# The first FFN of a decoder trunk as 2x2 block products in seven products, on one core

## The chip, the cores and the metric

The kernel runs on one core of one Trainium2 chip. The metric is the device time of one execution in microseconds (us). TensorE (PE) multiplies, VectorE (DVE), ScalarE (ACT) and GpSimd (POOL) work on SBUF, DVE and ACT also read PSUM, and SyncE (SP) issues the DMAs.

## The reference, cut to what matters

```python
def swiglu(u, wg, wu, wd):
    return (jax.nn.silu(u @ wg) * (u @ wu)) @ wd

x = x + 0.5 * swiglu(rms_norm(x, norm_ffn1[i]), ffn1_gate[i], ffn1_up[i], ffn1_down[i])
x = x + mixer(rms_norm(x, norm_mix[i]), ...)            # SSD scan and pooling heads
x = x + 0.5 * swiglu(rms_norm(x, norm_ffn2[i]), ffn2_gate[i], ffn2_up[i], ffn2_down[i])
gate = jax.nn.sigmoid(rms_norm(x, norm_ple[i]) @ ple_gate[i])
x = x + gate * (p[i] @ ple_proj[i])
y = rms_norm(x, final_norm)
```

There are 1024 prompt tokens and 32 sample tokens, together T = 1056. The model width is 1024, the FFN width 2816, all in float32.

## The kernel before

**Layout.** Features lie on the 128 partitions, tokens along the free axis. The width of 1024 is 8 row blocks (KB), the FFN width 22 blocks of 128 (NF). Tokens go in three chunks, `CH`, of 384, 384 and 288 columns.

**Precision.** Each operand is split into an upper and a lower part, rounded for TensorE (type fp32r). A product is three matmuls: upper by upper, lower weights by upper activations, upper weights by lower activations (`three`, whose matmul is line L280). For a weight tile ACT makes the upper part (L244) and DVE the lower (L245); for the activations of a norm ACT L307 and DVE L308 do it, with the norm's gain.

**The FFN** (`ffn`). The gate of a block is 3 chunks of 24 matmuls, then the up of the block is 3 chunks of 24, 144 in all. DVE L356 takes a gate chunk out of PSUM times the norm's factor R, ACT L357 applies SiLU, POOL L358 multiplies by R; DVE L368 takes the up chunk out, ACT L369 and DVE L370 split the result into g. The down projection goes in 8 `GROUPS` of 2 or 3 blocks between the gates and ups: a chunk is 6 or 9 matmuls, and DVE L387 adds it to x. Its 24 chunks by 8 groups make 192 evictions in each FFN.

**PSUM** is 8 banks of 512 columns, each a tile of its own. `bank()` hands out 7 of them in turn (5 in the scan).

**The start.** `start` runs the first block while x and the first weights still land: it goes block by block of the rows, with six banks open, and after each row the engines make the next operands. DVE and POOL add up the squares for the norm (L413); `finish_norm` (PE L322, ACT L323, DVE L325 to L327) makes R, which the first evictions need.

**Order.** PE's order is as the code is written (`MAN`); DVE, ACT and POOL are put in order by a scheduler except where the manual part of the program (`MS`) sets it. Weights come through a stream with `next_w`: one DMA of 512 KB (SP, L225) for each tile of gate or up, 256 or 384 KB for each pair of down tiles.

Of the kernel before, what the change touches and what calls it, by code (L numbers as in the profile page):

```python
# [78 lines left out]
def emit(tc, dr):  # L79
# [8 lines left out]
    # ---- SBUF: what stays for the whole run, and a pool for each phase  # L88
# [12 lines left out]
    o_X = new(sb, "X", 16 * T, F32R)     # [8][2][T], operands split in two parts  # L101
# [16 lines left out]
    banks = [pp.tile([P, 512], F32, name=f"bank{i}") for i in range(8)]  # L118
# [24 lines left out]
    # ---- the stream of weights, in the order of use  # L143
# [38 lines left out]
    ffn_stream("wgu1", "wd1")  # L182
# [68 lines left out]
    def first_w(q):  # L251
        """a quarter of the first two tiles"""
        for i in range(2):
            ap, n, _ = stream[i]
            o_r, o_w, k = raws[i] + n // 4 * q, where[i] + n // 4 * q, n // 4
            SY.dma_start(f(o_r, k), ap[:, k * q : k * q + k])
            S.copy(r(o_w, k), f(o_r, k))
            V.tensor_tensor(r(o_w + n, k), f(o_r, k), f(o_w, k), op=ALU.subtract)
            held[i] = i
            ready[i] = (where[i], n)  # L260
        st["made"], st["loaded"] = 2, 2
# [12 lines left out]
    def three(ps, terms):  # L274
        """ps = sum of w @ x over the terms ((wh, wl), (xh, xl)), without the product of the lower parts"""
# [65 lines left out]
    # ---- FFN  # L341
# [49 lines left out]
    # ---- FFN 1  # L391
    def start():
        for kb in range(KB):
            src = f(L["x"] + kb * T, T)
            if kb == 0:
                cuts = [(0, CH[0][1]), (CH[1][0], T - CH[1][0])]
            else:
                cuts = [(0, T)]
            for c0, n in cuts:
                SY.dma_start(src[:, c0 : c0 + n], dr["xT"][:, kb, c0 : c0 + n])  # L400
                if kb % 2 == 0 and c0 == 0:
                    first_w(kb // 2)
                split_gain(o_X + (2 * kb * T + c0), o_X + ((2 * kb + 1) * T + c0), src[:, c0 : c0 + n], vec(V_FFN1 + kb), n)
            acc = f(L["acc"], T)
            if kb == 0:
                S.activation(acc, src, AF.Square)
            else:
                sq = f((o_sq, o_T)[kb % 2], T)
                if kb in (1, 3):
                    V.tensor_tensor(sq, src, src, op=ALU.mult)  # L410
                else:
                    S.activation(sq, src, AF.Square)
                (G if kb < 5 else V).tensor_tensor(acc, acc, sq, op=ALU.add)  # L413
        SY.dma_start(f(o_cst, C_N), dr["cst"])
        V.tensor_copy(r(o_rii, P), cst(C_ID, P))
        V.tensor_copy(r(o_rii + P, P), cst(C_ID, P))
        wg, wu = next_ws(2)
        pss = [[bank()[:, 0:n] for c0, n in CH] for _ in range(2)]
        later_norm(o_R0, True)
        for kb in range(KB):  # L420
            for i, (p, q) in enumerate(((0, 0), (1, 0), (0, 1))):
                for w, pw in zip((wg, wu), pss):
                    for (c0, n), ps in zip(CH, pw):
                        PE.matmul(ps, lhsT=w(kb, p), rhs=Xs(kb, q, c0, n), start=kb == 0 and i == 0, stop=kb == KB - 1 and i == 2)  # L424
                if kb == KB - 1 and i < 2:
                    for c0, n in CH[i : 2 * i + 1]:
                        Rn(o_R0, c0, n)
        return pss

    o_sq = new(ph_acc, "sq", T)  # L430
# [6 lines left out]

    def done1(m, c0, n):
        src = f(L["x"] + m * T + c0, n)
        next_norm(o_R0, V_MIX, m, c0, n, src)  # L440
        if c0 + n == T:
            SY.dma_start(d_x[:, m, :], f(L["x"] + m * T, T))

    def before1():
        less_w(2)
        st["leaves"] = L["raw"]
        if L["raw"] in raws:
            raws.remove(L["raw"])

    ffn(o_R0, done1, start, before1)  # L450
# [3 lines left out]
    # ---- pooling heads  # L454
    ph_ffn.release()
# [6 lines left out]
    def pool_in(m):  # L462
# [678 lines left out]
```

## Time and profile before

| | |
|---|---|
| median of three runs | 2425.45 us (2424.33 to 2428.67) |
| span of the profiled execution | 2425.2 us |
| PE busy | 2350.8 us, 97% of the span |
| DVE busy | 1202.8 us, 50% |
| ACT busy | 680.9 us, 28% |
| POOL busy | 484.9 us, 20% |

The profiled execution is one of the kind that was timed; its span is 0.25 us below the median. The busy shares are means over the whole span: stages with different limits lie behind them. "PE" counts a matmul from its start to the end of its drain, so it can be busy and yet not at its best pace; the pace is read from a stretch divided by its matmuls.

### The profile page before, as it was taken

To read this page: it belongs to the slowest core of one execution; us is meant where nothing else is said; L and a number is where in the kernel's file an instruction comes from. 1 tells how busy PE (TensorE), PEld (TensorE's weight loads), DVE (VectorE), ACT (ScalarE), POOL (GpSimd) and SP (SyncE) were. 2 spreads that over 40 slices of the span, in tenths; PEclk is the share of its full clock that TensorE was granted. 3 is DMA by queue.
4 is the path that set the end of the run, shared out by engine and by line. 5 is a ranking of instruction groups with operands and counts; after the bars stand their busy time and mean duration, and the time that the engine had idled before them with its cause. 6 is when DMAs were issued, how large, how long until landed. Compare 5 with 4: busy or idle time off the path is not lost.

```text
span 2425.2 us, 34578 instructions
## 1 busy us (share of the span) xinstructions
PE 2350.8 (97%) x14259; PEld 2295.7 (95%) x14259; DVE 1202.8 (50%) x1912; ACT 680.9 (28%) x1132; POOL 484.9 (20%) x415
## 2 busy tenths in 40 slices
PE   8999999999999999999878999999999999999997
PEld 8999999999999999977767889999999999999997
DVE  7442433333245875555888774344333332433766
ACT  5111111111114224323443543311111112111555
POOL 3001000010103420013545435101000101000343
PEclk9999999999999999999999999999999999999999
DMA  4111111111112333344344664311111111111244
GB/s 151 49 57 39 54 40 46 51 42 53 38 44 89 75 92 70 52 124 138 113 144 133 186 185 128 127 53 57 40 46 51 44 50 38 49 48 44 64 140 130
DMA packets 135150, 192.36 MB, mean 79 GB/s; under 512 B 54672, under 2 KB 95952, under 8 KB 134992
## 3 DMA queue, kind: packets, MB, share of 16 engines
q1 hardware_dynamic: 134992, 190.15, 25.8%
q8 instruction: 112, 1.84, 0.3%
q14 instruction: 46, 0.38, 0.1%
HBM read 154.33 MB, written 35.78 MB: 78 GB/s over the span
## 4 chain that ended last, share of the span: by engine, by line
PE 85%; DVE 7%; ACT 2%; DMA 2%; issue 2%; POOL 1%; SPq 0%; DVEq 0%; POOLq 0%; ACTq 0%
PE bank L280 81%; PE bank L843 1%; DVE yol L821 1%; DVE X L308 1%; DVE wl L831 1%; PE bank L810 1%; ACT X L307 1%; DMA tmp<-d_z 1%; PE bank L424 1%; DMA x<-xT 1%; PE bank L322 0%; DVE x L387 0%; PE bank L747 0%; DVE W L245 0%; DVE Wa L687 0%
## 5 line engine op out<-in xcount | busy, mean ns | idle before, releaser
L280 PE MATMUL bank<-X,W 128*128 128x384 f32 (+1 forms) x9168 | 1505.7, 325 | 11.2 <-ACT X L882 4.6
L280 PEld LDWEIGHTS bank<-X,W 128*128 128x128 f32 x9168 | 1487.9, 189 | 16.6 <-ACT X L882 5.0
L280 PE MATMUL bank<-g,W 128*128 128x384 f32 (+1 forms) x3264 | 534.6, 324 | 2.1 <-ACT g L991 1.7
L280 PEld LDWEIGHTS bank<-g,W 128*128 128x128 f32 x3264 | 529.6, 188 | 2.9 <-ACT g L991 2.0
L358 POOL TENSOR_TENSOR tmp<-tmp,R 128x384 f32<-128x384 f32 x132 | 135.4, 1027 | 1302.7 <-ACT tmp L357 1302.7
L244 ACT CAST W<-raw 128x1024 fp32r<-128x1024 f32 (+2 forms) x230 | 211.1, 921 | 639.3 <-PE bank L280 608.9
L387 DVE SCALAR_TENSOR_TENSOR x<-bank,x 128x384 f32<-128x384 f32 (+1 forms) x384 | 198.6, 522 | 187.4 <-PE bank L280 187.3
L245 DVE TENSOR_TENSOR W<-raw,W 128x1024 fp32r<-128x1024 f32 (+2 forms) x230 | 250.1, 1090 | 65.0 <-ACT W L244 65.0
L356 DVE TENSOR_TENSOR tmp<-bank,R 128x384 f32<-128x384 f32 x132 | 68.9, 524 | 340.4 <-PE bank L280 340.3
L368 DVE TENSOR_TENSOR tmp<-bank,tmp 128x384 f32<-128x384 f32 x132 | 69.3, 525 | 289.3 <-PE bank L280 286.3
L369 ACT CAST g<-tmp 128x384 fp32r<-128x384 f32 x132 | 64.2, 487 | 342.8 <-DVE tmp L368 342.8
L357 ACT ACTIVATE tmp<-tmp 128x384 f32<-128x384 f32 x132 | 65.4, 498 | 328.1 <-DVE tmp L356 328.1
L316 POOL TENSOR_TENSOR acc<-acc,tmp 128x384 f32<-128x384 f32 (+1 forms) x82 | 84.2, 1035 | 94.7 <-ACT tmp L315 86.9
L280 PE MATMUL bank<-yh,W 128*128 128x384 f32 (+1 forms) x384 | 94.0, 330 | 0.0
L370 DVE TENSOR_TENSOR g<-tmp,g 128x384 fp32r<-128x384 f32 x132 | 68.9, 523 | 49.4 <-ACT g L369 49.4
L280 PEld LDWEIGHTS bank<-yh,W 128*128 128x128 f32 x384 | 68.5, 192 | 1.0 <-issue 0.6
L280 PE MATMUL bank<-yl,W 128*128 128x384 f32 (+1 forms) x192 | 62.6, 326 | 0.0
L308 DVE SCALAR_TENSOR_TENSOR X<-x,vec,X 128x384 fp32r<-128x384 f32 (+3 forms) x57 | 53.8, 949 | 17.1 <-ACT X L307 16.8
L650 DVE SCALAR_TENSOR_TENSOR cv<-xb,vec,cv 128x1080 f32<-128x1080 f32 x36 | 48.3, 1341 | 2.5 <-ACT cv L648 2.1
L787 POOL TENSOR_TENSOR Wa<-Wa,sm 128x1024 f32<-128x1024 f32 x16 | 49.5, 3092 | 0.0
L810 PE MATMUL bank<-xde,bt 128*128 128x512 f32 x32 | 20.9, 742 | 27.3 <-DVE xD L702 25.4
L307 ACT ACTIVATE X<-x,vec 128x384 fp32r<-128x384 f32 (+3 forms) x57 | 37.6, 661 | 31.7 <-DVE x L387 29.4
(230 smaller groups left out, 1600.9 us busy)
## 6 DMA issues: line engine op xcount, KB each, us to landing
raw<-wgu SPq DMA_DIRECT2D x86, 512.0 KB, 3.5
raw<-wd SPq DMA_DIRECT2D x48, 384.0 KB, 3.0
raw<-win SPq DMA_DIRECT2D x28, 512.0 KB, 4.9
raw<-ple SPq DMA_DIRECT2D x24, 512.0 KB, 3.7
Wa<-d_ac SPq DMA_DIRECT2D x16, 512.0 KB, 3.8
raw<-wout SPq DMA_DIRECT2D x16, 512.0 KB, 4.0
tmp<-d_x SPq DMA_DIRECT2D x32, 192.0 KB, 2.5
d_x<-tmp SPq DMA_DIRECT2D x32, 192.0 KB, 2.4
```

The costliest lines, as they stand in the source:

```text
L244: S.copy(r(o_w, n), f(o_r, n))
L245: V.tensor_tensor(r(o_w + n, n), f(o_r, n), f(o_w, n), op=ALU.subtract)
L280: PE.matmul(ps, lhsT=a, rhs=b, start=i == 0, stop=i == n - 1)
L308: V.scalar_tensor_tensor(r(o_lo, n), src, gain, f(o_hi, n), op0=ALU.mult, op1=ALU.subtract)
L316: eng.tensor_tensor(f(L["acc"] + c0, n), f(L["acc"] + c0, n), f(o_q, n), op=ALU.add)
L356: V.tensor_tensor(f(t, n), ps, Rn(o_R, c0, n), op=ALU.mult)
L357: S.activation(f(t, n), f(t, n), AF.Silu)
L358: G.tensor_tensor(f(t, n), f(t, n), f(o_R + c0, n), op=ALU.mult)
L368: V.tensor_tensor(f(t, n), ps, f(t, n), op=ALU.mult)
L369: S.copy(r(o_hi, n), f(t, n))
L370: V.tensor_tensor(r(o_lo, n), f(t, n), f(o_hi, n), op=ALU.subtract)
L387: V.scalar_tensor_tensor(xm, ps, 0.5, xm, op0=ALU.mult, op1=ALU.add)
```

## The change

**Seven products.** For one FFN block, gate and up over the two halves of the 1024 rows (weights) and the two halves of the tokens (528 each) are a 2x2 block product. Before it was 144 matmuls a block, of 384 and 288 columns. Now it is 7 products (`product`) of 24 matmuls of 264 columns (L451), 168 in a block; a product fills two banks, each with 4 pairs of row blocks by 3 matmuls. Operands are sums and differences: of the activations once, at the start (`operands`: seven pieces of 528 columns for each of 4 pairs of row blocks, each split in two), of the weights for each block (`make_unit`: POOL L434 to L436 add, ACT L439 and DVE L440 split; 8 slots for the units, one raw load of 1 MB for each block). The results are put together from three PSUM pairs by DVE (L474 to L488), after ACT has copied the first product out (L472).

**PSUM.** For the whole program the eight banks are now halves of four tiles of 1024 columns, `pairs`. `bank()` is as it was.

**Through HBM.** The FFN's result goes to `d_h` in HBM. After all 22 blocks `ffn_b` reads it back (`load_g`) and does the down projection in 4 `KGROUPS` of 5 or 6 blocks: 24 chunks of 15 or 18 matmuls each, 96 evictions (L544) in place of 192. x is loaded a second time.

The second FFN's code, the mixer's and the end's are unchanged but for the banks.

```diff
-    banks = [pp.tile([P, 512], F32, name=f"bank{i}") for i in range(8)]
+    pairs = [pp.tile([P, 1024], F32, name=f"bank{i}") for i in range(4)]
+    banks = [pairs[i // 2][:, 512 * (i % 2) : 512 * (i % 2) + 512] for i in range(8)]
+    d_h = dp.tile([P, NF, T], F32, name="d_h")
...
+    def operands(q, x1, x2, v_gain, o_b2, o_nd, o_u, o_e, o_f):
+
+        g1, g2 = vec(v_gain + 2 * q), vec(v_gain + 2 * q + 1)
+        u, e, fq, b2, nd = f(o_u, TH), f(o_e, TH), f(o_f, TH), f(o_b2, T), f(o_nd, T)
+        parts(0, q, x1[:, 0:TH], g1)
+        S.activation(b2, x2, AF.Copy, scale=g2)
+        G.tensor_tensor(u, x1[:, 0:TH], x1[:, TH:T], op=ALU.subtract)
+        V.scalar_tensor_tensor(e, u, g1, b2[:, TH:T], op0=ALU.mult, op1=ALU.add)
+        parts(1, q, e)
+        parts(2, q, b2[:, 0:TH])
+        V.scalar_tensor_tensor(nd, x1, g1, b2, op0=ALU.mult, op1=ALU.subtract)
+        G.tensor_tensor(fq, nd[:, TH:T], nd[:, 0:TH], op=ALU.subtract)
+        parts(3, q, nd[:, TH:T])
+        parts(4, q, u, g1)
+        parts(5, q, fq)
+        parts(6, q, b2[:, TH:T])
...
+        if u == 0:
+            G.tensor_tensor(f(o_s, 1024), f(o_raw, 1024), f(o_raw + 512, 1024), op=ALU.add)
+            G.tensor_tensor(f(o_s + 1024, 512), f(o_raw + 1024, 512), f(o_s, 512), op=ALU.add)
+            G.tensor_tensor(f(o_s + 1536, 512), f(o_raw + 1536, 512), f(o_s + 1024, 512), op=ALU.add)
+        where_, c = U_SRC[u]
+        src, o = (o_raw if where_ == "raw" else o_s) + c, unit_at(i)
+        S.copy(r(o, 512), f(src, 512))
+        V.tensor_tensor(r(o + 512, 512), f(src, 512), f(o, 512), op=ALU.subtract)
+        if u == 5 and fb + 1 < NF:
+            load_raw(a, fb + 1)
+
+    def product(pair, o, i, first):
+        w = unit_at(i)
+        for h in range(2):
+            ps = pair[:, 512 * h : 512 * h + CQ]
+            for q in range(4):
+                x = piece(o, q) + CQ * h
+                for j, (p, b) in enumerate(((0, 0), (1, 0), (0, 1))):
+                    PE.matmul(ps, lhsT=r(w + (512 * p + P * q), P), rhs=r(x + TH * b, CQ),
...
+        for fb in range(NF):
+            o_g, o_c, o_u1, o_u2 = (L7["cg"] + ((fb % 2) * 4 + k) * TH for k in range(4))
+            for s in range(7):
+                i = 7 * fb + s
+                product(pairs[(0, 1, 0, 1, 2, 1, 2)[s]], s, i, s in (0, 1, 4))
+                if fb == 0 and s == 0:
+                    for c0, n in CH:
+                        Rn(o_R, c0, n)
+                make_unit(a, i + NU)
+                if s == 0:
+                    S.copy(p1, pa)
+                elif s == 1:
+                    V.tensor_tensor(v2, p1, px, op=ALU.subtract)
...
```

**Three places of the order.** The rows stand in the order in which an engine goes through them; "waits" names the engines whose signals the row waits for, and "x5" stands for five equal rows. On PE, in the down projection of the second FFN, before (bank_74 to bank_81 are the eight PSUM tiles, each one bank):

```order
L280 MATMUL bank_80<-g_11605,W_72 128x384 [waits DVE_49]
L280 MATMUL bank_80<-g_11605,W_72 128x384 x5
L280 MATMUL bank_74<-g_11605,W_72 128x384 [waits DVE_49]
L280 MATMUL bank_74<-g_11605,W_72 128x384 x5
L280 MATMUL bank_75<-g_11605,W_72 128x288 [waits DVE_49]
L280 MATMUL bank_75<-g_11605,W_72 128x288 x5
```

The same place now (bank_74 to bank_77 are the four pairs, each with two banks):

```order
L274 MATMUL bank_74<-g_12395,W_72 128x384 x6
L274 MATMUL bank_74<-g_12395,W_72 128x288 [waits DVE_49]
L274 MATMUL bank_74<-g_12395,W_72 128x288 x5
L274 MATMUL bank_75<-g_12395,W_72 128x384 x6
L274 MATMUL bank_75<-g_12395,W_72 128x384 [waits DVE_49]
L274 MATMUL bank_75<-g_12395,W_72 128x384 x5
L274 MATMUL bank_76<-g_12395,W_72 128x288 x6
L274 MATMUL bank_76<-g_12395,W_72 128x384 [waits DVE_49,Activation_49]
L274 MATMUL bank_76<-g_12395,W_72 128x384 x5
L274 MATMUL bank_77<-g_12395,W_72 128x384 x6
```

Before, each chunk's first matmul waited for the eviction that had emptied its own bank seven chunks earlier. Now the first chunk of a pair has no wait for DVE, and the second waits; the signal's count that is compiled into that wait is that of the eviction of the chunk just ahead, in the other half of the same tile.

On ACT, in the loop over the FFN's blocks, before (W are weight tiles, raw what was loaded, tmp a chunk of the gate or up, g the result):

```order
L357 ACTIVATE tmp_69<-tmp_69 128x384 [waits DVE_49] x2
L244 CAST W_12_93<-raw_14_95 128x1024 [waits DMAHW7_49,PE_49,Activation_49]
L357 ACTIVATE tmp_69<-tmp_69 128x288 [waits DVE_49]
L369 CAST g_92<-tmp_69 128x384 [waits DVE_49] x2
L244 CAST W_13_94<-raw_70 128x1024 [waits DMAHW0_49,PE_49,Activation_49]
```

And now (ws are the sums of weights that POOL makes, cg the FFN's results, p the copy of the first product):

```order
L439 CAST W_14_116<-ws_117 128x512 [waits PE_49,Pool_49]
L439 CAST W_14_116<-raw_70 128x512 [waits DMAHW1_49,PE_49,Activation_49]
L490 ACTIVATE cg_121<-cg_121 128x528 [waits Pool_49]
L439 CAST W_14_116<-ws_117 128x512 [waits PE_49,Activation_49,Pool_49]
L472 COPY p_16_118<-bank_74 128x528 [waits Activation_49]
L439 CAST W_14_116<-raw_70 128x512 [waits PE_49]
```

A cast that waits for the next block's load, and a cast that waits for POOL's sums of that load, now stand ahead of the copy that empties the first product's pair.

On POOL, at the start, before (acc is the norm's sum; the rows after these belong to the first gate):

```order
L413 TENSOR_TENSOR acc_99<-acc_99,tmp_69 128x1056 [waits DVE_49,Activation_49]
L413 TENSOR_TENSOR acc_99<-acc_99,sq_115 128x1056 [waits Activation_49,Pool_49]
L413 TENSOR_TENSOR acc_99<-acc_99,tmp_69 128x1056 [waits DVE_49,Pool_49]
L413 TENSOR_TENSOR acc_99<-acc_99,sq_115 128x1056 [waits Activation_49,Pool_49]
```

And the first rows now (p_16 and n_18 hold u and f of `operands`, cg the rows of x), which go on to 21 rows before the norm: 8 of L407 and L412, 6 of L434 to L436 and 7 of L572:

```order
L407 TENSOR_TENSOR p_16_118<-cg_121 128x528 [waits DMAHW1_49]
L572 TENSOR_TENSOR acc_106<-acc_106,tmp_69 128x1056 [waits Activation_49]
L412 TENSOR_TENSOR n_18_120<-nd_108 128x528 [waits DVE_49]
L434 TENSOR_TENSOR ws_117<-raw_70 128x1024 [waits DMAHW3_49]
L435 TENSOR_TENSOR ws_117<-raw_70,ws_117 128x512 [waits Pool_49]
L436 TENSOR_TENSOR ws_117<-raw_70,ws_117 128x512 [waits Pool_49]
L407 TENSOR_TENSOR p_16_118<-cg_121 128x528 [waits DMAHW5_49,DVE_49]
L572 TENSOR_TENSOR acc_106<-acc_106,tmp_69 128x1056 [waits Activation_49]
```

POOL had four additions there and has 21, eight of them in the chain from x to the operands of the products.

## Rows read from the trace of the kernel before

**Rows 1.** The page: span, busy time by engine, last chain by engine.
```profile
span 2425.2 us, 34578 instructions
PE 2350.8 (97%) x14259; PEld 2295.7 (95%) x14259; DVE 1202.8 (50%) x1912; ACT 680.9 (28%) x1132; POOL 484.9 (20%) x415
PE 85%; DVE 7%; ACT 2%; DMA 2%; issue 2%; POOL 1%; SPq 0%; DVEq 0%; POOLq 0%; ACTq 0%
```
**Rows 2.** Windows: stretch, length, busy PE, PEld, DVE, ACT, POOL, clock, DMA, GB/s.
```profile
41.46:786.49 745.03, 745.03 (x4610) 745.03 (x4610) 288.89 (x486) 151.93 (x248) 85.69 (x83) 1.00 0.15 50
1433.39:2289.00 855.61, 855.28 (x5285) 854.32 (x5284) 338.72 (x557) 193.92 (x319) 129.75 (x129) 1.00 0.19 61
```
**Rows 3.** Last chain's pieces: start, length, what.
```profile
41.46 730.71 PE bank L280 x4518
...
1144.82 2.38 PE bank L843 x20
...
1519.58 4.21 PE bank L280 x24
1524.44 3.17 PE bank L280 x24
```
**Rows 4.** Groups by shape: count, busy us, mean ns of one, idle before.
```profile
L280 PE MATMUL bank<-X,W 128*128 128x384 f32 x6120 | 1103.9, 338 | 1.2 <-DVE xb L642 0.7 <-DVE X L308 0.3
...
L387 DVE SCALAR_TENSOR_TENSOR x<-bank,x 128x384 f32<-128x384 f32 x256 | 142.1, 555 | 128.6 <-PE bank L280 128.5
L358 POOL TENSOR_TENSOR tmp<-tmp,R 128x384 f32<-128x384 f32 x88 | 89.8, 1022 | 1213.9 <-ACT tmp L357 1213.9
...
L387 DVE SCALAR_TENSOR_TENSOR x<-bank,x 128x288 f32<-128x288 f32 x128 | 58.3, 455 | 58.8 <-PE bank L280 58.8
...
L809 POOL TENSOR_TENSOR xD<-xD,xd 128x512 f32<-128x512 f32 x14 | 18.0, 1287 | 30.0 <-DVE xd L808 30.0
...
L245 DVE TENSOR_TENSOR W<-raw,W 128x512 fp32r<-128x512 f32 x20 | 14.3, 713 | 0.8 <-ACT W L244 0.8
...
L244 ACT CAST W<-raw 128x512 fp32r<-128x512 f32 x20 | 12.4, 620 | 28.4 <-PE bank L280 16.7 <-issue 8.6 <-DMA raw<-poolw 3.2
...
L308 DVE SCALAR_TENSOR_TENSOR X<-tmp,vec,X 128x384 fp32r<-128x384 f32 x16 | 9.9, 618 | 25.3 <-ACT X L307 25.3
...
L899 ACT COPY tmp<-bank 128x384 f32<-128x384 f32 x16 | 7.6, 478 | 30.2 <-PE bank L280 30.0
```
**Rows 5.** Timeline of the start, DVE and POOL: start, length, engine, what.
```profile
9.91 4.76 DVE L308 SCALAR_TENSOR_TENSOR X<-x,vec,X 128x1056 fp32r<-128x1056 f32 x2
10.14 3.41 POOL L413 TENSOR_TENSOR acc<-acc,tmp 128x1056 f32<-128x1056 f32 x1 [9.17 <-DVE tmp L410]
...
14.59 3.00 DVE L258 TENSOR_TENSOR W<-raw,W 128x256 fp32r<-128x256 f32 x2
...
29.33 1.30 DVE L308 SCALAR_TENSOR_TENSOR X<-x,vec,X 128x1056 fp32r<-128x1056 f32 x1
```
**Rows 6.** Timeline where PE starts again after a wait.
```profile
2287.59 1.37 DVE L308 SCALAR_TENSOR_TENSOR X<-x,vec,X 128x384 fp32r<-128x384 f32 x1
...
2289.01 0.44 PE L280 MATMUL bank<-X,W 128*128 128x384 f32 x1 [0.34 <-DVE X L308]
...
2289.29 0.69 PE L280 MATMUL bank<-g,W 128*128 128x384 f32 x3
```
**Rows 7.** Timeline of the first norm, its first and last step.
```profile
37.59 0.81 PE L322 MATMUL bank<-acc,cst 128*128 128x384 f32 x2
...
42.38 0.92 DVE L327 SCALAR_TENSOR_TENSOR R<-acc,R 128x384 f32<-128x384 f32 x2
```
**Rows 8.** DMA issues: count, KB each, median us from issue to landing.
```profile
raw<-wgu SPq DMA_DIRECT2D x86, 512.0 KB, 3.5
...
raw<-wd SPq DMA_DIRECT2D x16, 256.0 KB, 2.6
```
**Rows 9.** PE after idle times in the scan: timeline, then the window's clock.
```profile
1277.59 2.77 PE L280 MATMUL bank<-X,W 128*128 128x288 f32 x10 [3.44 <-DVE X L883]
...
1277.60:1280.30 2.70, 2.70 (x11) 2.70 (x12) 1.04 (x3) 0.10 (x1) 0.00 (x0) 0.50 0.55 153
```

More of the change, by code (lines that the diff above doesn't have):

```diff
@@ L30 @@
 XCB = 3 + TP + NB * (3 + NS)
+TH = T // 2
+CQ = TH // 2
+NU = 8
+KGROUPS = [range(0, 5), range(5, 11), range(11, 16), range(16, 22)]
+KSLOTS = [range(0, 5), range(8, 14), (5, 6, 7, 0, 1), range(8, 14)]
 GROUPS = [[0, 1], [2, 3], [4, 5, 6], [7, 8, 9], [10, 11, 12], [13, 14, 15], [16, 17, 18], [19, 20, 21]]
@@ L249, in make_w @@
         load_w()
[L251 to L261, printed above, removed]
     def next_ws(k):
@@ L389, in ffn @@
                                 done(m, c0, n)
[L392 to L396, printed above, removed]
-            else:
[L398 to L428, printed above, removed]
@@ L430, in emit, with piece, parts @@
-    o_sq = new(ph_acc, "sq", T)
+    L7 = {}
+    def piece(o, q):
+        i = 4 * o + q
+        return o_X + 2 * TH * i if i < 16 else L7["E"] + 2 * TH * (i - 16)
+    def parts(o, q, src, gain=None):
+        hi, lo = piece(o, q), piece(o, q) + TH
+        if gain is None:
+            S.copy(r(hi, TH), src)
+            V.tensor_tensor(r(lo, TH), src, f(hi, TH), op=ALU.subtract)
+        else:
+            split_gain(hi, lo, src, gain, TH)
+    def operands(q, x1, x2, v_gain, o_b2, o_nd, o_u, o_e, o_f):
[13 more added lines that the diff above has]
+        parts(6, q, b2[:, TH:T])
@@ new lines, in emit, with unit_at, load_raw, make_unit @@
+    U_SRC = (("raw", 1024), ("sums", 1024), ("raw", 1536), ("sums", 512), ("sums", 0), ("raw", 0), ("sums", 1536))
+    def unit_at(i):
+        k = i % NU
+        return o_W + 1024 * k if k < 4 else L7["W2"] + 1024 * (k - 4)
+    def load_raw(a, fb):
+        SY.dma_start(f(o_raw, 2048), flat(a, fb * P * 2048, 2048))
+    def make_unit(a, i):
+        fb, u = divmod(i, 7)
+        if fb >= NF:
+            return
+        o_s = L7["sums"]
+        if u == 0:
[8 more added lines that the diff above has]
+            load_raw(a, fb + 1)
@@ new lines, in product, with two @@
+    def product(pair, o, i, first):
[6 more added lines that the diff above has]
+                    PE.matmul(ps, lhsT=r(w + (512 * p + P * q), P), rhs=r(x + TH * b, CQ),
+                              start=first and q == 0 and j == 0, stop=q == 3 and j == 2, skip_group_check=not first)
+    def two(ap):
+        return ap.rearrange("p (b n) -> p b n", b=2)
@@ new lines, in emit, with down_w, load_down, make_down @@
+    B = {}
+    def down_w(i):
+        k = i % 4
+        return (o_W + 2048, L7["W2"], L7["W2"] + 1536, o_W)[k]
+    def load_down(a):
+        i = B["loaded"]
+        if i < 8 * len(KGROUPS):
+            n = len(KGROUPS[i // 8]) * P
+            SY.dma_start(f(o_raw + 1024 * (i % 2), n), flat(a, B["at"], n))
+            B["at"] += P * n
+            B["loaded"] += 1
+    def make_down(a):
+        i = B["made"]
+        if i < 8 * len(KGROUPS):
+            n = len(KGROUPS[i // 8]) * P
+            src, o = f(o_raw + 1024 * (i % 2), n), down_w(i)
+            S.copy(r(o, n), src)
+            V.tensor_tensor(r(o + n, n), src, f(o, n), op=ALU.subtract)
+            B["made"] += 1
+            load_down(a)
@@ new lines, in g_slot, with load_g, ffn_b @@
+    def g_slot(k):
+        return o_X + 2 * T * k if k < 8 else L7["E"] + 2 * T * (k - 8)
+    def load_g(d_in, fb, k):
+        o, src = g_slot(k), f(L7["hraw"] + T * (fb % 2), T)
+        SY.dma_start(src, d_in[:, fb, :])
+        S.copy(r(o, T), src)
+        V.tensor_tensor(r(o + T, T), src, f(o, T), op=ALU.subtract)
+    def ffn_b(a, d_in, x, done):
+        for gi, (grp, slots) in enumerate(zip(KGROUPS, KSLOTS)):
+            if gi + 1 < len(KGROUPS):
+                for fb, k in zip(KGROUPS[gi + 1], KSLOTS[gi + 1]):
+                    load_g(d_in, fb, k)
+            n_ = len(grp) * P
+            for m in range(8):
+                w = down_w(8 * gi + m)
+                for c0, n in CH:
+                    ps = bank()[:, 0:n]
+                    three(ps, [((r(w + j * P, P), r(w + (n_ + j * P), P)), (r(g_slot(k) + c0, n), r(g_slot(k) + (T + c0), n)))
+                               for j, k in enumerate(slots)])
+                    xm = f(x(m) + c0, n)
+                    V.scalar_tensor_tensor(xm, ps, 0.5, xm, op0=ALU.mult, op1=ALU.add)
+                    if gi == len(KGROUPS) - 1:
+                        done(m, c0, n)
+                make_down(a)
@@ new lines, in emit @@
+    ph_acc, ph_st = phase("sums", "right"), phase("start", "right")
+    L["acc"], o_b2, o_nd = new(ph_acc, "acc", T), new(ph_st, "b2", T), new(ph_st, "nd", T)
+    ph_ffn, ph = phase("ffn"), phase("ffn_a")
+    L7["E"], L7["W2"] = new(ph_ffn, "E", 12 * 2 * TH, F32R), new(ph_ffn, "W2", 4096, F32R)
+    L7["sums"] = new(ph, "ws", 2048)
+    L7["p1"], L7["v2"], L7["n3"] = (new(ph, n_, TH) for n_ in ("p1", "v2", "n3"))
+    L7["cg"] = new(ph, "cg", 8 * TH)
+    for q in range(4):
+        xs_ = [f(L7["cg"] + (2 * q + j) % 4 * T, T) for j in range(2)]
+        for j in range(2):
+            SY.dma_start(xs_[j], dr["xT"][:, 2 * q + j, :])
+        if q == 0:
+            load_raw("wgu1", 0)
+        operands(q, *xs_, V_FFN1, o_b2, o_nd, L7["p1"], L7["v2"], L7["n3"])
+        for j in range(2):
+            acc = f(L["acc"], T)
+            if q + j == 0:
+                S.activation(acc, xs_[j], AF.Square)
+            else:
+                sq = f(o_T, T)
+                S.activation(sq, xs_[j], AF.Square)
+                G.tensor_tensor(acc, acc, sq, op=ALU.add)
+        if q == 0:
+            SY.dma_start(f(o_cst, C_N), dr["cst"])
+            V.tensor_copy(r(o_rii, P), cst(C_ID, P))
+            V.tensor_copy(r(o_rii + P, P), cst(C_ID, P))
+            for i in range(NU):
+                make_unit("wgu1", i)
@@ new lines, in emit, with tail @@
+    later_norm(o_R0, True)
+    ph_st.release()
+    ph_hr = phase("hraw", "right")
+    L7["hraw"], o_x0 = new(ph_hr, "hraw", 2 * T), new(ph_hr, "x0", T)
+    SY.dma_start(f(o_x0, T), dr["xT"][:, 0, :])
+    B.update(made=0, loaded=0, at=0)
+    def tail(s):
+        if s == 0:
+            load_down("wd1")
+            load_down("wd1")
+            make_down("wd1")
+            load_g(d_h, 0, 0)
+            load_g(d_h, 1, 1)
+        elif s == 2:
+            make_down("wd1")
+            load_g(d_h, 2, 2)
+            load_g(d_h, 3, 3)
+        elif s == 3:
+            make_down("wd1")
+            load_g(d_h, 4, 4)
+        elif s == 6:
+            make_down("wd1")
@@ L436, in next_norm @@
             later_norm(o_R)
+    ph.release()
+    ph = phase("ffn_b")
+    o_x = [o_x0] + [new(ph, f"x{m}", T) for m in range(1, 8)]
+    for m in range(1, 8):
+        SY.dma_start(f(o_x[m], T), dr["xT"][:, m, :])
     def done1(m, c0, n):
-        src = f(L["x"] + m * T + c0, n)
-        next_norm(o_R0, V_MIX, m, c0, n, src)
+        next_norm(o_R0, V_MIX, m, c0, n, f(o_x[m] + c0, n))
         if c0 + n == T:
[L442 to L450, printed above, removed]
+            SY.dma_start(d_x[:, m, :], f(o_x[m], T))
+    ffn_b("wd1", d_h, lambda m: o_x[m], done1)
+    ph.release()
+    ph_hr.release()
+    ph_ffn.release()
     ms = tc.manual_schedule(engines=MS)
     ms.__enter__()
-    ph_ffn.release()
     ph_pd = phase("pooled")
@@ L1089, in ffn, with seven @@
         return w, np.concatenate(parts)
+    def seven(g, u, d):
+        g, u = (w.reshape(4, 2, P, NF, P).transpose(3, 2, 1, 0, 4) for w in (g, u))
+        w = np.concatenate([u[:, :, ::-1], g], 2)
+        db = d.reshape(NF, P, 8, P)
+        parts = [np.ascontiguousarray(db[grp[0] : grp[-1] + 1].transpose(2, 1, 0, 3)).reshape(-1) for grp in KGROUPS]
+        return np.ascontiguousarray(w).reshape(-1), np.concatenate(parts)
     col = lambda v: np.ascontiguousarray(v.reshape(-1, P).T)
-    wgu1, wd1 = ffn(a["ffn1_gate"][0], a["ffn1_up"][0], a["ffn1_down"][0])
+    wgu1, wd1 = seven(a["ffn1_gate"][0], a["ffn1_up"][0], a["ffn1_down"][0])
     wgu2, wd2 = ffn(a["ffn2_gate"][0], a["ffn2_up"][0], a["ffn2_down"][0])
```

32 lines of the change are left out of this document (27 added, 5 removed).

## The prediction, made before the changed kernel was run

> **What bounds the kernel now.** I read the page first. Of a span of 2425.2 us PE is busy for 97%, and the last chain lies 85% on PE [rows 1]. The span is 0.25 us below the median of the runs, so a sum against it and a forecast of the median differ by that much. Then the windows: from 41.46 to 786.49 us, the rest of the first FFN after its first block, PE is busy for all of 745.03 us at a granted clock of 1.00 (the 2.4 GHz level). It runs 4610 matmuls there, 161.6 ns each. The stretch of the second FFN, 1433 to 2289, reads the same, with DVE busy for 339 of 856 us [rows 2]. The chain says it in another way: one piece of 730.71 us, 4518 matmuls in which PE waits for nothing [rows 3]. So in both FFNs the time is the number of matmuls times their pace. A matmul saved counts in full, but only as long as nothing makes PE stand still. A stall of PE counts in full too.
>
> **The products.** Before, a block's gate and up are 144 matmuls, 144 x 161.6 ns = 23.27 us. Now they are 168 of 264 columns. The trace has none of that width. Its neighbours are 20 of 256 columns in 2.38 us (119.0 ns each) and 24 of 288 in 3.17 us (132.1) [rows 3]; a quarter of the way between them is 122.3 ns. A block is 168 x 122.3 = 20.55 us, 2.72 less. The first block belongs to the start, so 21 blocks give **-57 us** (bounds: -69 at 119.0 ns, -23 at 132.1). Seven products for eight save 12.5% of the columns, but shorter matmuls and their fixed part give some back: 24 of 384 take 4.21 us, 175.4 ns [rows 3].
> The Trainium skill, "TensorE: Matmul & The Clock Gate", section "Back-to-back issue gap", gives a warm matmul its columns at 2.4 GHz and about 2.5 ns more, which would be 109 ns for 256 columns and 112.5 for 264. The row with 256 columns shows 119.0, so the measurement decides; by the page the sum would be 36 us lower.
>
> **The pair tiles.** This is the largest term. The order shows that the second chunk in a pair waits for DVE: for the eviction of the chunk just ahead, which sits in the other half of the same tile. Before, the wait was for an eviction seven chunks back, long over. PE is in order: everything behind that matmul stands. I counted 238 such waits in the whole order (82 in the second FFN's down projection, 56 in its gates and ups, 42 in the first's down, 58 in the rest), 3 in each 7 chunks. Some ten have other work between; I take 228, 161 behind a chunk of 384 columns and 67 behind one of 288.
> The price is a chain. The last matmul drains: one takes 338 ns alone, its pace is 175 [rows 4, 3], so 0.16. DVE evicts, 0.555 or 0.455 us [rows 4]. PE starts 0.055 us after DVE's end (2287.59 + 1.37 = 2288.96, next matmul at 2289.01) and the matmul after that comes 0.28 later, 0.105 over its pace [rows 6]. With 0.01 for DVE's start it is 0.89 or 0.79 us, 161 x 0.89 + 67 x 0.79 = 196. DVE may be in the middle of other work: its 40% share [rows 2] adds some hundredths each. I take **+205 us** (bounds: 180 at 0.79 each, 320 if each also waits half a microsecond).
>
> **The start.** Before, block 0 is done at 41.46 us [rows 2]. Now all operands pass DVE and POOL first. The timeline shows that two operations that touch SBUF alone do not run side by side on these two: L308's two of 1056 columns take 4.76 us around POOL's 3.41, while one alone takes 1.30 [rows 5]. So I add the two engines up. DVE: 12 multiplications of 528 columns at 0.765 (between 0.618 for 384 [rows 4] and 1.30 for 1056), 4 of 1056 at 1.30, 20 subtractions at 0.70 and 8 of the units at 0.68 (both from 0.713 for 512), 34.3 us with 0.4 for the constants. POOL: 1.022 for 384 and 1.287 for 512 columns [rows 4] make 2.07 ns a column; 8 of 528 at 1.31, 7 of 1056 at 2.43 and two sets of sums at 4.93 are 37.4 us. Add 4 us until the first data, 5 for the norm (37.59 to 43.30 before, partly under products [rows 7]), 1.5 of handoffs: product 2 starts at about 82. PE has idled, so its first microseconds are at the lower clock, as after the gap in [rows 9]: one product at half pace, 3 us. Six products of 24 x 122.3 ns = 2.94 us follow, 17.6: block 0 is done at 102.6, **+61 us**. Bounds: +29 if half of POOL's work overlaps DVE's, +71 if every handoff of the 56 operations costs 0.2 more.
>
> **The ring of weights.** ACT takes its rows in order: a cast that waits for the next block's load, SiLU that waits for POOL, a cast that waits for POOL's sums, then the copy that empties the first product's pair. PE's third product of a block waits for that copy. The load itself starts only when the sixth unit of the block has been split, which waits for product 5, whose slot it takes. From the end of product 5: drain 0.16, eviction on DVE 0.71 (slope from 288 to 384 columns, 1.04 ns each [rows 4]), split 0.68, load of 1 MB 5.3 (3.5 us for 512 KB and 2.6 for 256 [rows 8], so 1.8 more), POOL's sum 2.37, the split beside it 0.68, POOL's product and second sum 1.32 and 1.29, cast 0.62 and copy 0.60 (from 0.478 for 384 [rows 4]), handoffs 0.3: 14.0 us. PE has four products in that time, 11.74 us. It stands 2.3 us a block, 20 blocks: **+46 us**. Bounds: nothing, at a load of 3.5 us; +100, at 2 x 3.5 = 7.0 and one more POOL operation ahead.
>
> **The rest.** The down projection keeps its 1584 matmuls. x and the FFN's result through HBM lie under them: DMA is busy 15% in that stretch [rows 2], and each group's 5 or 6 reloads have 64 us (396 x 161.6 ns); without that cover each would cost its load, 3.5 us or more. At the end of the first FFN the next weight tile waits for the last down matmul, since its slot is in use: cast and split of 1024 columns, twice 0.62 and 0.71, with handoffs, **+5** (0 to 10). The scan's chunks in pairs: **+4** (0 to 25).
>
> **Sum.** 2425.2 - 57 + 205 + 61 + 46 + 5 + 4 = 2689, with 0.25 to the median about **2690 us**. This case alone: 2640 to 2745.
>
> **The rivals.**
> *B, no stall in the ring*: the load takes 3.5 us as one of 512 KB does, or ACT's scheduler order costs less. The DMA queues are idle 85% of that stretch, which speaks for it; twice the bytes speak against. 2644 us.
> *C, the clock falls at the ring's gaps.* After 3.44 us of idling ten matmuls ran at a granted clock of 0.50, the 1.2 GHz level [rows 9]. If a product of each block does, it takes twice its 2.94 us, 20 times: +59, 2749 us. Against it, the gaps I expect are shorter.
> *D, the evictions queue.* The eviction that PE waits for finds a weight split of 1024 columns (1.4 us by the 512 row) ahead of it on DVE and waits half a microsecond more: 228 x 0.5 = +114, 2804 us. DVE's 40% speaks for some of it.
> *F, the start overlaps*: DVE and POOL block each other less than by rows 5: -32, 2658 us.
> *G, the pair waits cost PE nothing*: the two halves are different banks, and PE would write one while DVE reads the other. -205, 2485 us. Against it: PE obeys the signal that the order prints, whatever the memory allows. The Trainium skill, "PSUM — Partial Sum Buffer", section "Summary: rules for kernel authors", says to target a different bank while PSUM is read and to guard with semaphores by bank; by that rule these waits need not be there, but the guard here is by tile. No row here shows such a wait.
> *E, not slower*: the 264-column matmul is much faster than its neighbours. There are 22 x 168 = 3696 of them, so each ns is 3.7 us. To make up 265 us it must fall by 72 ns, to 50; at or below that the change is not slower. The rows at 119.0 and 132.1 speak against it.
>
> **How the numbers follow.** Forecast 0.61, B 0.10, C 0.10, D 0.09, F 0.05, G 0.02, E 0.03. The predicted time is the forecast's, 2690. The range 2610 to 2790 takes in B, C, F and the bounds of the start and the ring; it leaves out D, G, E and the forecast's tails, some 0.18. A difference under 0.2% (5 us) can't be told from none. Only E ends on that side: faster 0.02, same 0.01, slower 0.97.
>
> **What the changed profile would show.** In the second FFN the windows should show PE below 90%, by 138 idle pieces of about 0.55 to 0.9 us before matmuls of the down, gate and up lines, released by DVE's evictions; the stretch should be some 120 us longer than 856. If it is not, the largest term is wrong. The seven-product part should have 122 ns a matmul, and an idle piece of about 2 us in each block before the third product, released by ACT's copy; its own releaser should be the cast of the sums. Block 0 should be done near 103 us, with DVE and POOL taking turns before. A pace of 132 ns, a start under 75 us, or a ring without idle time would each move the time by the bounds given.

## The result, and the profile after

The changed kernel takes 2818.65 us (2818.02 to 2819.28, four runs), the kernel before 2425.46: a ratio of 1.162, 95% interval 1.160 to 1.164. It is 393 us slower, 129 more than forecast and outside the range. The profiled execution spans 2816.9 us.

The page of the changed kernel; its lines answer to the first two of [rows 1]:

```profile
span 2816.9 us, 35938 instructions
PE 2402.0 (85%) x14787; PEld 2267.5 (80%) x14787; DVE 1310.5 (47%) x1898; ACT 743.6 (26%) x1219; POOL 723.3 (26%) x536
```

PE is busy 51 us longer than before, but the span grew by 392: most of the loss is PE standing still. Windows by stage show where. First the changed kernel (block 0; the other gates and ups; the first FFN's down projection; pooling heads and projection; scan; the second half of w_out; second FFN; end), with the columns of [rows 2]:

```profile
0.00:96.94 96.94, 35.80 (x197) 30.90 (x198) 72.45 (x66) 42.95 (x62) 49.44 (x29) 0.63 0.25 89
96.94:561.70 464.76, 436.33 (x3530) 431.90 (x3529) 246.45 (x274) 131.21 (x213) 268.16 (x164) 1.00 0.23 80
561.70:867.30 305.60, 270.25 (x1587) 258.13 (x1586) 112.49 (x169) 63.70 (x95) 26.69 (x25) 0.99 0.28 92
867.30:1205.50 338.20, 290.06 (x1692) 275.57 (x1692) 179.30 (x240) 76.04 (x101) 44.14 (x38) 0.96 0.26 56
1205.50:1625.40 419.90, 332.96 (x1738) 283.72 (x1739) 271.21 (x444) 154.17 (x301) 157.53 (x106) 0.89 0.43 135
1625.40:1739.00 113.60, 100.37 (x583) 96.51 (x582) 40.87 (x65) 33.41 (x60) 43.85 (x45) 0.97 0.33 108
1739.00:2649.30 910.30, 807.64 (x4762) 766.99 (x4762) 307.18 (x510) 170.31 (x274) 89.17 (x87) 1.00 0.14 46
2649.30:2816.90 167.60, 128.61 (x709) 123.79 (x707) 80.51 (x134) 71.86 (x116) 44.33 (x43) 0.89 0.31 102
```

The last five stages in the kernel before:

```profile
786.49:1062.80 276.31, 273.53 (x1693) 268.76 (x1692) 182.36 (x246) 79.40 (x108) 47.83 (x42) 1.00 0.34 69
1062.80:1423.30 360.50, 314.71 (x1764) 271.50 (x1764) 265.44 (x442) 153.08 (x300) 158.89 (x106) 0.95 0.50 156
1423.30:1519.58 96.28, 93.14 (x559) 92.17 (x560) 43.56 (x68) 35.59 (x62) 43.81 (x45) 0.96 0.42 133
1519.58:2289.00 769.42, 769.09 (x4756) 768.40 (x4754) 302.08 (x502) 162.74 (x264) 87.01 (x85) 1.00 0.16 53
2289.00:2425.20 136.20, 120.69 (x709) 116.85 (x709) 87.83 (x143) 74.77 (x124) 47.71 (x45) 0.94 0.43 135
```

These five run the same matmuls as before (9484 records in all, before 9481; the cut between the scan and w_out lies some 25 matmuls, 4 us, apart in the two) and lost 61.9, 59.4, 17.3, 140.9 and 31.4 us, 311 of the 392. The first FFN, which is what the change is about, lost 81: the start 96.94 - 41.46 = 55.5, its down projection 305.6 - 1584 x 161.6 ns = 49.6, while the 21 blocks of gates and ups won 489.0 - 464.8 = 24.

What PE waited for, from the lists of waits of the second FFN, the pooling stage, the scan, w_out and the end (waiter, releaser: us in all, times, longest):

```profile
PE bank L274 <- DVE x L378: 60.0, 82, 2.2
PE bank L274 <- DVE tmp L347: 21.5, 29, 3.4
PE bank L274 <- DVE tmp L359: 20.0, 28, 0.7
...
PE bank L274 <- DVE pa L651: 18.3, 6, 8.1
PE bank L274 <- DVE xb L816: 9.4, 10, 1.4
PE bank L274 <- ACT ys L691: 8.6, 9, 2.4
PE bank L274 <- DVE pa L653: 5.4, 5, 2.7
...
PE bank L274 <- DVE xb L818: 1.4, 2, 0.7
...
PE bank L1019 <- DVE xd L984: 21.3, 13, 5.9
...
PE bank L274 <- DVE tmp L1146: 13.2, 11, 4.4
...
PE bank L274 <- DVE tmp L1213: 22.2, 9, 6.1
```

In the second FFN before, PE waited for nothing; now it waits 139 times for an eviction, where I had counted 138 in the order. One of them in the timeline:

```profile
1832.18 0.46 DVE L378 SCALAR_TENSOR_TENSOR x<-bank,x 128x288 f32<-128x288 f32 x1 [1.15 <-PE bank L274]
1833.23 0.56 DVE L378 SCALAR_TENSOR_TENSOR x<-bank,x 128x384 f32<-128x384 f32 x1 [0.59 <-PE bank L274]
1833.84 2.10 PE L274 MATMUL bank<-g,W 128*128 128x384 f32 x12 [0.65 <-DVE x L378]
```

DVE starts its eviction at 1833.23, when PE has ended the chunk (1833.84 - 0.65 = 1833.19), and PE starts the next chunk 0.05 us after that eviction has ended: the chain of the prediction. In the pooling stage the same wait is longer:

```profile
901.07 4.65 DVE L666 TENSOR_TENSOR ps<-ps 128x1184 f32<-128x1184 f32 x2
...
905.75 3.07 DVE L673 SCALAR_TENSOR_TENSOR ps<-ps,pa 128x1024 f32<-128x1024 f32 x1
...
911.79 0.55 DVE L651 TENSOR_TENSOR pa<-bank,R 128x384 f32<-128x384 f32 x1
912.40 1.01 PE L274 MATMUL bank<-X,W 128*128 128x384 f32 x2 [7.62 <-DVE pa L651]
```

The eviction L651 stands behind the pooling heads' own sums on DVE. With seven banks that delay had no one waiting for it: PE's longest wait in this stage was 0.7 us before. With a pair, PE waits 7.62 us.

### The profile page after: what moved, and what is told of

Read it like the earlier page. It is cut to its first block, busy times and chain, and to the rows that moved or that the text cites. A ratio compares the mean times of both kernels' runs of the same rounds, so it can differ in the third digit from the quotient of the medians.

```text
span 2816.9 us, 35938 instructions
## 1 busy us (share of the span) xinstructions
PE 2402.0 (85%) x14787; PEld 2267.5 (80%) x14787; DVE 1310.5 (47%) x1898; ACT 743.6 (26%) x1219; POOL 723.3 (26%) x536
## 5 line engine op out<-in xcount | busy, mean ns | idle before, releaser
L274 PE MATMUL bank<-X,W 128*128 128x384 f32 (+1 forms) x6864 | 1181.5, 331 | 144.9 <-DVE tmp L347 21.5
L274 PE MATMUL bank<-g,W 128*128 128x384 f32 (+1 forms) x1680 | 297.0, 329 | 61.4 <-DVE x L378 57.2
L274 PEld LDWEIGHTS bank<-g,W 128*128 128x128 f32 x1680 | 270.2, 188 | 86.0 <-DVE x L378 74.6
L451 PE MATMUL bank<-X,W 128*128 128x264 f32 x2112 | 273.2, 289 | 74.0 <-ACT p L472 26.0
L451 PEld LDWEIGHTS bank<-X,W 128*128 128x128 f32 x2112 | 264.6, 191 | 80.6 <-ACT p L472 30.3
L250 ACT CAST W<-raw 128x1024 fp32r<-128x1024 f32 (+3 forms) x156 | 142.2, 914 | 540.6 <-PE bank L274 512.8
L451 PE MATMUL bank<-E,W 128*128 128x264 f32 x1584 | 197.2, 285 | 2.4 <-DVE n L480 2.4
L251 DVE TENSOR_TENSOR W<-raw,W 128x1024 fp32r<-128x1024 f32 (+3 forms) x156 | 169.8, 1091 | 59.5 <-ACT W L250 59.5
L451 PEld LDWEIGHTS bank<-E,W 128*128 128x128 f32 x1584 | 194.9, 188 | 2.6 <-DVE n L480 2.6
L274 PE MATMUL bank<-E,W 128*128 128x384 f32 (+1 forms) x864 | 145.1, 326 | 14.1 <-DVE x L544 13.0
L274 PEld LDWEIGHTS bank<-E,W 128*128 128x128 f32 x864 | 139.1, 188 | 20.0 <-DVE x L544 13.6
L544 DVE SCALAR_TENSOR_TENSOR x<-bank,x 128x384 f32<-128x384 f32 (+1 forms) x96 | 50.2, 523 | 158.4 <-PE bank L274 154.4
L440 DVE TENSOR_TENSOR W<-ws,W 128x512 fp32r<-128x512 f32 x88 | 73.3, 834 | 62.3 <-ACT W L439 62.2
L439 ACT CAST W<-ws 128x512 fp32r<-128x512 f32 x88 | 54.5, 620 | 154.4 <-PE bank L451 141.5
L440 DVE TENSOR_TENSOR W<-raw,W 128x512 fp32r<-128x512 f32 x66 | 90.8, 1376 | 9.2 <-ACT W L439 9.1
```

The costliest lines, as they stand in the source:

```text
L274: PE.matmul(ps, lhsT=a, rhs=b, start=i == 0, stop=i == n - 1)
L439: S.copy(r(o, 512), f(src, 512))
L440: V.tensor_tensor(r(o + 512, 512), f(src, 512), f(o, 512), op=ALU.subtract)
L451: PE.matmul(ps, lhsT=r(w + (512 * p + P * q), P), rhs=r(x + TH * b, CQ), start=first and q == 0 and j == 0, stop=q == 3 and j == 2, skip_g ...
L544: V.scalar_tensor_tensor(xm, ps, 0.5, xm, op0=ALU.mult, op1=ALU.add)
```

## The experiments

**e1: pairs for the seven products alone.**

```diff
-    pairs = [pp.tile([P, 1024], F32, name=f"bank{i}") for i in range(4)]
-    banks = [pairs[i // 2][:, 512 * (i % 2) : 512 * (i % 2) + 512] for i in range(8)]
+    last_two = [pp.tile([P, 512], F32, name=f"bank{i}") for i in (6, 7)]
+    pq = [tc.alloc_tile_pool(name="pq", bufs=1, space=PSUM, reuse_waits="tile")]
+    pairs = [pq[0].tile([P, 1024], F32, name=f"pair{i}") for i in range(3)]
+    banks = [None] * 6 + last_two
...
     ffn_a("wgu1", o_R0, d_h, tail)
+    pq.pop().release()
+    pq.append(tc.alloc_tile_pool(name="pr", bufs=1, space=PSUM, reuse_waits="tile"))
+    banks[0:6] = [pq[0].tile([P, 512], F32, name=f"bank{i}") for i in range(6)]
...
```

> The changed kernel with pair tiles only while the seven products run; afterwards six banks of 512 columns are tiles of their own again, and the last two always are. Theory (pair tiles): all that was lost behind the first FFN, 311 us in the windows, and some 44 of the 49 us lost in its down projection come from the waits for the chunk just ahead; without them the time is 2818.65 - 355 = 2463 us, and the second FFN takes 769 us again. Rival (the mixer and the end lose time through something else in the change, such as the shortened weight stream, the scheduler's order or the DMA scratch): only the waits I counted go, 238 at about 1.0 us, and the time is about 2580, with the pooling heads, the scan and the end still some 110 us longer than before.

Measured: 2459.74 us, ratio to before 1.0145 (1.0129 to 1.0161), 359 us less than the changed kernel. The theory said 2463, the rival 2580. What else the change did to the program (its shortened weight stream, the DMA scratch) is still in e1, so it is not what cost these 359 us. All the waits that PE has left in the second FFN are one:

```profile
PE bank L276 <- DVE X L301: 0.3, 1, 0.3
```

**e2: the kernel before with pairs.** One part of the change alone:

```diff
-    banks = [pp.tile([P, 512], F32, name=f"bank{i}") for i in range(8)]
+    pairs = [pp.tile([P, 1024], F32, name=f"bank{i}") for i in range(4)]
+    banks = [pairs[i // 2][:, 512 * (i % 2) : 512 * (i % 2) + 512] for i in range(8)]
```

> The kernel before with one part of the change alone: its eight banks as halves of four tiles. Theory (pair tiles): behind the first FFN it loses the same 311 us as the changed kernel, and in the first FFN another 138 waits at 1.02 us, 141; 2425 + 452 = 2877 us. Rival (something else in the change costs the mixer and the end their 110 us): 334 waits at about 1.0 us, about 2755.

Measured: 2896.99 us in one run, 470 more than the kernel before beside it (2426.86); the theory's 2877 is 20 too low, the rival's 2755 is far off. Its waits repeat the list above, with both FFNs in the first three rows:

```profile
PE bank L281 <- DVE x L388: 119.8, 160, 2.3
PE bank L281 <- DVE tmp L357: 44.3, 58, 4.3
PE bank L281 <- DVE tmp L369: 41.6, 57, 1.1
```

With e1 this settles it: the two lines that cut PSUM into four tiles cost 359 us in the changed kernel and 470 in the kernel before, while e1, which keeps the rest of the change and pairs for the seven products alone, is 33 us slower than the kernel before.

**e3: the raw weights in two loads**, on top of e1:

```diff
...
-        if u == 5 and fb + 1 < NF:
-            load_raw(a, fb + 1)
+        if u in (2, 5) and fb + 1 < NF:
+            load_raw(a, fb + 1, int(u == 2))
...
```

> As e1, and a block's raw weights come as two loads of 512 KB, each started when its half is free: the second half already after the third unit. Theory (the ring's last link is the load of 1 MB): the idle time before the third product, 26 us in all in the trace, goes; e1 - 26, about 2437 us. Rival (the stall is ACT's order, a cast behind POOL's sums, whatever the load does): the idle pieces stay above 1 us, e1 - 0 to 5, about 2460.

Measured: 2496.65 us, 37 slower than e1: neither the theory's time nor the rival's. The idle piece before the third product of a block grew from about 1.27 to 2.33 us. Its timeline:

```profile
187.60 2.39 POOL L436 TENSOR_TENSOR ws<-raw 128x1024 f32<-128x1024 f32 x1
190.06 1.62 POOL L437 TENSOR_TENSOR ws<-raw,ws 128x512 f32<-128x512 f32 x1
191.76 1.29 POOL L438 TENSOR_TENSOR ws<-raw,ws 128x512 f32<-128x512 f32 x1
193.01 1.31 POOL L491 TENSOR_TENSOR cg<-cg,R 128x528 f32<-128x528 f32 x1
194.36 0.64 ACT L492 ACTIVATE cg<-cg 128x528 f32<-128x528 f32 x1 [5.78 <-POOL cg L491]
194.91 0.60 ACT L441 CAST W<-ws 128x512 fp32r<-128x512 f32 x1
195.41 0.59 ACT L474 COPY p<-pair 128x528 f32<-128x528 f32 x1
196.06 7.07 PEld L453 LDWEIGHTS pair<-X,W 128*128 128x128 f32 x45 [2.54 <-ACT p L474]
```

The scheduler now put all three sums of weights ahead of L491 on POOL; in the changed kernel, and in e1 too, the same multiplication (L489 and L491 there) stood between the first and the second sum. ACT's SiLU waits for it, and the copy stands behind the SiLU on ACT. So the chain ended through POOL's and ACT's order. This is read from the trace; that order was not tried by itself, so e3 does not price the load either. 20 pieces of 1.06 us more are 21 us; the rest is, as far as the trace tells, the clock: 10 of the 20 double products (48 matmuls in a row) behind these pieces took 1.5 us longer (last section).

**e4: a start without POOL**, on top of e3:

```diff
...
-        G.tensor_tensor(u, x1[:, 0:TH], x1[:, TH:T], op=ALU.subtract)
+        V.tensor_tensor(u, x1[:, 0:TH], x1[:, TH:T], op=ALU.subtract)
...
+            eng = V if i < NU else G
...
-                G.tensor_tensor(acc, acc, sq, op=ALU.add)
+            for c0, n in CH:
+                PE.matmul(sums[c0], lhsT=cst(C_ONE, P), rhs=sq[:, c0 : c0 + n], start=2 * q + j == 0, stop=2 * q + j == 7)
...
```

> As e3, and at the start POOL does nothing: its differences and the first block's sums go to DVE, and the norm's sum over the rows is made by PE as a product with ones of each row's squares. Theory (DVE and POOL take turns at the start, so their times add up): 37 us of POOL's turns become 11 on DVE, the norm is off the tail, the first block is done at about 72 us and not 97; e3 - 25, about 2412 us. Rival (the start is held by the loads of x or by ACT, whose work there is 43 us): less than 8 us gained, about 2430.

Measured: 2473.96 us, 22.7 less than e3. Block 0 is done at 68.4 us, 3.6 before the 72 expected; in e3 it was done at 93.9. The window shows POOL nearly gone and DVE busy for less than in the changed kernel's 72.45, though it has more to do (80 instructions for 66):

```profile
0.00:68.42 68.42, 45.90 (x238) 37.49 (x239) 51.80 (x80) 41.79 (x62) 3.64 (x9) 0.85 0.37 126
```

The 20 subtractions of 528 columns that split the operands took DVE 1.41 us each in the changed kernel's start and 0.70 us here: next to POOL's work they took twice as long. e4 changed two things at once, since PE now also adds up the norm; how much of the 22.7 us each is worth was not measured.

**e5: time for the copy**, on top of e1:

```diff
...
+    SEQ = (0, 1, 4, 3, 2, 5, 6)
...
-            for s in range(7):
-                i = 7 * fb + s
+            for k, s in enumerate(SEQ):
+                i = 7 * fb + k
...
```

> As e1 (one load of 1 MB), with the products of a block in the order 0, 1, 4, 3, 2, 5, 6 in place of 0 to 6, and the units made in that order: the product that adds to the first pair comes four places after the one before it, so the copy of the first product no longer has to be done within one product. Theory (the stall is ACT's order: SiLU and a cast behind POOL stand ahead of the copy): with two products more to hide it, the 26.7 us of idle time before the third product go; e1 - 26, about 2434 us. Rival (the ring of loads and sums itself takes longer than seven products, whatever the order): the stall moves to another product, and the time stays near 2460.

Measured: 2429.53 us, ratio to before 1.0018 (1.0008 to 1.0027), 30 less than e1. Of the 26.7 us that PE waited for the copy nothing is left; three waits for DVE, 2.5 us together, are all that the list has for the blocks. Most blocks look like this, without idle time:

```profile
81.16 6.02 PE L454 MATMUL pair<-X,W 128*128 128x264 f32 x48
87.02 6.02 PE L454 MATMUL pair<-E,W 128*128 128x264 f32 x48
92.88 6.02 PE L454 MATMUL pair<-X,W 128*128 128x264 f32 x48
98.74 3.09 PE L454 MATMUL pair<-E,W 128*128 128x264 f32 x24
101.67 6.02 PE L454 MATMUL pair<-X,W 128*128 128x264 f32 x48
```

The first row and the last are the same products of two blocks, so a block takes 101.67 - 81.16 = 20.51 us. The ring of loads and sums fits into that, though the load of 1 MB takes 4.8 us as in e1; it was the copy's place.

**e6: e5 with the start of e4.**

> e5 with the start of e4 (no work on POOL there, the norm's sums on PE). Theory (start and ring are independent terms): e4 was 23 us faster than e3, so e5 - 23, about 2411 us, and below the kernel before by 0.6%. Rival (the gain at the start is given back in the ring, since block 1's weights are then late): e5 - 10 or less, about 2425, no faster than before.

Measured: 2410.2 us, ratio to before 0.9943 (0.9929 to 0.9957): 0.6% faster, a small difference, but the interval lies below 1. The kernel before kept its own start, and e5, with seven products and the start as changed, only comes within 0.2% of it; so the 0.6% belongs to e6 as a whole. It is 19.3 below e5, near the theory's 23: block 0 is done 23.2 us earlier (69.7 for 92.9), and some of that is lost again behind it. One of the start's waits is new: the norm's third sum sits in the third pair, which the third product now takes early, and PE waits 3.86 us for it:

```profile
53.45 4.66 PE L456 MATMUL pair<-E,W 128*128 128x264 f32 x24 [3.86 <-DVE acc L319]
```

## Why the prediction was wrong, step by step

**The products** (-57). Right. 48 matmuls start 5.86 us apart in e5, 122.1 ns each; I had 122.3 between two rows. A block takes 20.51 us where I had 20.55. The Trainium skill, "TensorE: Matmul & The Clock Gate", section "Back-to-back issue gap", gives the formula that I used, N/2.4 + 2.5 ns, as the gap of an isolated matmul; for 264 columns it comes to an estimate of 112.5 ns. The trace does not agree, and the row was the better guide. The section says itself that a stream of weight loads and matmuls does not follow that formula, so the 36 us that I worked out from it were no forecast by the page.

**The start** (+61). Right in mechanism and nearly in size: block 0 is done at 96.9 us for 102.6, +55.5. That DVE and POOL slow each other there is what e4 shows (1.41 us a subtraction for 0.70). Some 4 us had another cause: in e1, whose start differs only in the banks, block 0 is done at 92.2. The norm's sums shared a pair in the changed kernel, and PE waited 1.26 us twice between them; in e1 the three run without a wait.

**The ring** (+46). The mechanism held, the size was too large. PE waits 26.0 us in 20 pieces for ACT's copy, as the chain said, and the blocks lost 34 us in all against 20.51 a piece. The load of 1 MB took 4.8 us, not 5.3:

```profile
raw<-wgu SPq DMA_DIRECT2D x22, 1024.0 KB, 4.8
```

I named ACT's order as part of the chain and then priced it by the load; e5, with the same load, shows that the order of the products decides whether PE feels it.

**The down projection and the handoff** (42 waits and +5, 43 us in all). The first FFN's down projection lost 49.6 us, with 40 waits for its evictions. In e1 it takes 259.0 us, so all but 3.0 of that came from the tiles.

**The pair tiles** (+205). This is the step that failed: "58 in the rest", at the same 0.9 us as in the FFNs, with +4 for the scan. In the second FFN the step was right, 139 waits and 140.9 us, 1.01 each for the 0.9 taken. In the pooling heads, the scan, w_out and the end I had 56 us, and they lost 170; these 114 us are most of the 129 by which the forecast was short. Three things were wrong with it.

The count took only waits for DVE's eviction of the chunk just ahead. ACT's evictions (L691, 9 waits) and the scan's other tenants of a pair (L1019 on L984, 13 waits of 1.6 us, none before) were not in it.

The price took an eviction that is next on its engine. In the list above 43 waits for DVE's evictions outside the scan (L651, L653, L816, L818, L1146, L1213) come to 69.9 us, 1.6 us of idle time each; in the second FFN it is 0.73. Behind the pooling sums the eviction is not next (18.3 us in 6 waits). At the end, the chunk's eviction L1213 stands behind ACT's sigmoid (L1212) and, on DVE, behind a split of weights (L251):

```profile
2672.20 0.51 ACT L1212 ACTIVATE tmp<-tmp 128x384 f32<-128x384 f32 x1
2672.32 1.23 DVE L251 TENSOR_TENSOR W<-raw,W 128x1024 fp32r<-128x1024 f32 x1 [0.50 <-ACT W L250]
...
2673.47 0.55 DVE L1213 TENSOR_TENSOR tmp<-bank,tmp 128x384 f32<-128x384 f32 x1
...
2674.07 1.36 PE L274 MATMUL bank<-X,g 128*128 128x384 f32 x5 [1.86 <-DVE tmp L1213]
```

PE ended its chunk at 2672.21, the sigmoid ended at 2672.71 and the split at 2673.55. A split lies between the chunk's end and L1213 in all nine waits (22.2 us, 2.5 each). I read DVE's 40% share of the second FFN as if it held for stages where DVE has more to do: it is 74% in the scan (265 of 360 us before).

And the sum had no term for the clock behind these waits. In the windows above the granted clock falls from 1.00 to 0.96 in the pooling stage, from 0.95 to 0.89 in the scan and from 0.94 to 0.89 at the end. The missing share of the clock times the length, over the four stages, is 82 us after and 30 before; so by estimate at most some 50 of the 170 us are matmuls at the lower level (1.2 GHz). No run separates them from the waits themselves.

The waits are behind all of it: e1 gives back 359 us by the tiles alone, and after the first FFN it loses 7 us to the kernel before where the changed kernel lost 311 (2460.8 - 815.5 against 2425.2 - 786.5, spans less the end of the first FFN).

**The rivals.** D came nearest in time (2804), but not as I had put it, the same half microsecond everywhere. In the second FFN only some 16 of the 139 evictions stood behind other work on DVE, which comes to 0.1 us a wait on average; at the end it was every one, and a few places elsewhere cost several us each. That its sum comes near is chance. G is refuted: PE obeys the wait that was compiled, and e1 and e2 price it at 359 and 470 us. The Trainium skill, "PSUM — Partial Sum Buffer", section "Summary: rules for kernel authors", asks for a guard by bank; with tiles of one bank, as in e1, these waits are gone, so the trace agrees. B and F did not happen: the ring's pieces are there, and block 0 was done 26 us later than by F. E did not: 122.1 ns is far from 50. C did not happen in the changed kernel's blocks, whose clock reads 1.00 in spite of 20 pieces; it came in e3.

## What to carry to other kernels

In this program a tile was the unit of waiting. With two accumulators in one tile, a writer of the one waits for the reader of the other, in all code that shares the tile; so cut PSUM by what is evicted together, and give the pieces back when that phase is over. A wait that was slack before must be priced at each place by what stands ahead of the releaser on its engine there, not by the cheapest place, and the clock behind it must be looked at too. And where an in-order engine has a copy that PE waits for, give that copy time by the order of the products before making its neighbours faster.

## What the runs showed of the hardware beyond that

The 20 idle pieces before the third product, 1.2 to 1.8 us each, left the clock alone in e1 (1.00 over its blocks). With pieces of 2.2 to 2.5 us in e3, 10 of the 20 double products behind them ran part of the time at the lower level; the windows of two of them, one hit and one not:

```profile
148.31:155.81 7.50, 7.50 (x48) 7.50 (x49) 3.99 (x5) 1.73 (x3) 3.23 (x3) 0.77 0.35 108
172.95:178.92 5.97, 5.97 (x48) 5.97 (x49) 4.00 (x5) 1.73 (x3) 3.24 (x3) 1.00 0.43 130
```

Each hit cost 1.5 us, so such a stall cost more than its own length. And twice as many bytes in one load took less than the prediction's slope said: 4.8 us for 1 MB against 3.6 for 512 KB in the same run, where the slope gave 5.3.
